# One decoder block on one core: products with norm factors, splits of the gates' fourth sums and the groups of weight sums placed at other points of the program

## The chip, the cores and the metric

The kernel runs on one core of one Trainium2 chip. The metric is the device time of one execution in microseconds. Its work lies on TensorE (PE: matmuls; PEld: loads of stationary weights), VectorE (DVE), ScalarE (ACT), GpSimd (POOL, which here fills buffers and issues software DMAs) and SyncE (SP, which issues the loads and the small stores in the order of its queue).

## The reference

One layer of a decoder on 512 tokens and 16 learned meta tokens in front of them, width 1024, float32:

```
u   = rmsnorm(x) @ w_in          # one projection for both mixers
o   = hgrn2(q, f, i) of 8 heads  # S_t = diag(f_t) S_(t-1) + (1 - f_t) i_t^T,  o_t = S_t^T q_t
o   = o * rsqrt(mean(o*o, of the head) + EPS) * norm_w * silu(g)
y   = mamba2(z, x, B, C, dt)     # 16 heads, 2 groups, gated norm
x   = x + concat(o, y) @ w_out
a,b = split(causal_conv3(rmsnorm(x) @ w_up))      # 2 x 2816
out = rmsnorm(x + (silu(a) * b) @ w_down), without the meta tokens
```

The change touches how o is normed and gated, how the weights of g and of w_up are prepared, and where their parts stand in the program.

## The kernel before, in words

Everything is kept with features on the 128 partitions and tokens along the row. Each float32 operand of a product is split into hi and lo parts, and a product is three matmuls into one accumulator: hi x hi, hi x lo, lo x hi (`product`, L327 to L341, and `mul`, L958 to L965). A weight block of 128 x 1024 takes this way: SyncE loads it into one of three `raw` buffers (L266 to L275 and L294), ScalarE copies it, rounded, into `whi` (L212), VectorE subtracts that from `raw` into `wlo` (L213), TensorE reads both. `ahead` keeps the stream two blocks ahead of its use, in the order of the list `chunks`.

The stages are: projection and Mamba mixer (to about 205 us), HGRN heads 0 to 7 (to about 412), the gates g0 to g3 (to about 487), the output rows (to about 530), the up products (to about 755), the down products. The output rows' first halves (`add_row`) are computed among the HGRN heads, behind heads 1 and 2 (`ROWS`).

*Sums of weights and of tokens.* Gates and most up pairs use a scheme of seven products instead of eight half-size products (L980 to L1021 for a gate, `scheme` for a pair, called W). It needs sums of weight halves and sums of token halves. The weights' sums are made in DRAM by accumulating software DMAs of GpSimd (`weight_sums`, L232 to L258): for each pair, copies, two rounds of adds and a last one. The pairs are worked off in GROUPS, and each group starts on a *tick*: VectorE copies one element of a named tile, GpSimd waits for it. The three 256-wide column blocks of a scheme's weights come through `raw` (w0, w2, w1); the fourth sum, 512 wide, has a tile of its own, s4, loaded on SyncE (L273) and split by `split_half` into s4h on ScalarE and s4l on VectorE (L221, L222). The tokens' sums (`normed_sums` with `token_sums`: `un`, `t_u`, t0, t1) are four sets, k = 0 to 3, and are made behind the HGRN heads that USUMS names.

*An HGRN head* (`hgrn_head`) takes three projections (f, q, v), makes decays and the decayed copies of q and k on VectorE (the last of them is kC, L816), and then small products: v and k transposed into pv, pk, pm and copied out by ScalarE (vt L830, mt L829, kt L831, mt's masked part by VectorE, L854), state updates (S), and o. mt is read by TensorE at L835 and L867.

*The norm of o.* Behind heads 3 and 7, `hgrn_norm` squares four heads' o, sums over features on TensorE, takes logarithm and exponential on ScalarE (with table loads), writes the factors of each head to DRAM (rs_d, L891) and reads them back over all partitions (rb, L893), both on SyncE. `hgrn_scale` multiplies o by the factor and the norm's weight, four instructions on VectorE (L898): for heads 0 to 3 behind head 4, for heads 4 to 7 behind gate 0.

*A gate* g_i serves heads 2i and 2i+1: banks x and z (pgt), y and v (pyvg for gate 0, pyg and pvg later). x takes w0's first half; y is seeded from x (L970, ScalarE); x goes on with w0's second half; y takes w2's first half; z is seeded from y (L970); v, z and y take the other halves; VectorE adds (sgv, L1016 and L1017), ScalarE takes silu (L1018); z takes s4 (h4, l4); silu of x and z (L1021); o is multiplied by both and split (oa_hi, oa_lo).

*What sets the order.* Each engine has its own queue and runs it in order. The order is found by a list scheduler with a model of durations. What is written under `first()` has priority; `tc.issue_after(x)` keeps instructions from being placed ahead of x; otherwise the place in the program decides among what is ready. Buffers with a tag are handed out in rings: a tile's first writer waits until the last reader of the tile that held the buffer is done.

Of the kernel before, what the change touches and what calls it, by code (L numbers as in the profile page):

```python
# [19 lines left out]
T0 = META - 2  # L20
# [36 lines left out]
NG = NH // 2  # L57
GROUPS = [("g", i) for i in range(NG)], WS[0:5], WS[5:10], WS[10:13], WS[13:], [("dn", 1)], [("dn", 2)], [("dn", 3)]
HT = 258
USUMS = {4: (0,), 5: (1, 2), 6: (3,)}  # L60
ROWS = {1: range(0, 4), 2: range(4, 8)}
# [6 lines left out]
def tile_block(ctx: ExitStack, tc: tile.TileContext, xT, w_in, w_dt, w_out, w_up, w_down,  # L68
# [148 lines left out]

    last_s4 = []

# [40 lines left out]
    def scheme_weights(key):  # L260

        kind, j = key
        raw = raw_tile(key)
        hi, lo = split_tiles(key)
        if kind == "w0":
            nc.sync.dma_start(raw[:], pair_of(j)[0])  # L266
        elif kind == "w2":
            nc.sync.dma_start(raw[:], sumd[j][:, 0:2 * HK])
        else:
            n = "_".join(map(str, j)) if isinstance(j, tuple) else j  # L270
            tag = "m" if isinstance(j, tuple) else "ab"
            s4 = slot(f"s4_{n}", 512, tag=tag)
            nc.sync.dma_start(s4[:], sumd[j][:, 3 * HK:])  # L273
            nc.sync.dma_start(raw[:, 0:HK], sumd[j][:, 2 * HK:3 * HK])
            nc.sync.dma_start(raw[:, HK:], pair_of(j)[1][:, HK:])  # L275
        split_weights(raw, hi, lo, slice(0, 2 * HK), V)
        if kind != "w1":
            return hi, lo
        h4, l4 = slot(f"s4h_{n}", 512, F32R, tag=tag), slot(f"s4l_{n}", 512, F32R, tag=tag)
        last_s4[:] = [split_half(s4[:], h4[:], l4[:])]  # L280
        return hi, lo, h4, l4

    def ahead(n):
        while wnext[0] < min(n, len(chunks)):
            key, src, kc = chunks[wnext[0]]
            if key[0] in ("w0", "w1", "w2"):
                with first():
                    wdone[key] = scheme_weights(key)
                wnext[0] += 1
                continue  # L290
            with first(), ExitStack() as st:
                raw, hi, lo = raw_tiles(key)
                d = slice(0, kc * P)
                nc.sync.dma_start(raw[:, d], src() if callable(src) else src)  # L294
                if key[0] == "dn" and key[1] < 2 and not key[2]:
                    st.enter_context(tc.issue_after(last_s4[0].ins))
                split_weights(raw, hi, lo, d, V)
            wdone[key] = (hi, lo)
            wnext[0] += 1
# [314 lines left out]
    def mamba_heads(g):  # L614
# [4 lines left out]
        def decays(h):  # L619
# [11 lines left out]
            if h == 1:  # L631
                weight_sums(GROUPS[6], L)

# [73 lines left out]
    mamba_states(0)  # L707
    weight_sums(GROUPS[5], rstd1)
    next_phase(LOGS)
# [44 lines left out]
    os_ = []  # L754
    weight_sums(GROUPS[1], ys[7])

    def hgrn_head(h):
# [52 lines left out]
        def packed(t, c):  # L810
            return t.rearrange("p (a c t) -> p a c t", c=c, t=16)
# [3 lines left out]
        V.tensor_tensor(packed(qC, 4), vw(q_, 128, 64), part(1, 8, 4), ALU.mult)  # L815
        V.tensor_tensor(packed(kC, 4), vw(k_, 128, 0), part(4, 8, 0), ALU.mult)  # L816

# [76 lines left out]

    def hgrn_scale(h0):
        for h in range(h0, h0 + 4):
            o, rb = os_[h], rbs[h]
            V.scalar_tensor_tensor(o[:, T0:], o[:, T0:], col(C_HN + h), rb[:, T0:], ALU.mult, ALU.mult)  # L898

# [34 lines left out]
    def normed_sums(k):  # L934

        fs = []
        for kk in (k, k + KD // 2):
            t = slot(f"un{kk}", tag="L")
            V.tensor_tensor(t[:, T0:], uh[kk][:, T0:].bitcast(F32), ul[kk][:, T0:].bitcast(F32), ALU.add)
            fs += [t[:, c] for c in tails]  # L940
        uts.append(token_sums(f"u{k}", fs, "L", lambda: next(uplaces)))

    for h in range(NH):
        hgrn_head(h)
        for j in ROWS.get(h, ()):
            add_row(j, 1, obh, obl)
            if j == 3:
                weight_sums(GROUPS[2], hs[j])
        if h == 4:
            hgrn_scale(0)  # L950
        if h % 4 == 3:
            hgrn_norm(h - 3)
        for k in USUMS.get(h, ()):
            normed_sums(k)
        if h == 4:
            weight_sums(GROUPS[3], os_[h])

# [9 lines left out]
    def seed(ps, of):  # L967

        with evac():
            A.activation(ps, of, AF.Copy)  # L970

# [11 lines left out]
    for i in range(NG):  # L983
# [23 lines left out]
        mul(y, w2h[:, 0:HK], w2l[:, 0:HK], t2)  # L1007
        seed(z, y)
        w1h, w1l, h4, l4 = weights("w1", key)
        mul(v, w1h[:, 0:HK], w1l[:, 0:HK], t3, True)  # L1010
# [4 lines left out]
        with evac():  # L1015
            V.tensor_tensor(sv[:, B_], s7[:], z, ALU.add)  # L1016
            V.tensor_tensor(sv[:, A_], s7[:], y, ALU.add)  # L1017
            A.activation(sv[:], sv[:], AF.Silu, scale=-1.0)  # L1018
# [3 lines left out]
        for h, g in ((2 * i, sg), (2 * i + 1, sv)):  # L1022
# [8 lines left out]
            oal.append(lo)  # L1031
        if i == 0:
            hgrn_scale(4)
    weight_sums(GROUPS[4], os_[6])

# [159 lines left out]
    for j in range(KF):  # L1195
# [10 lines left out]
        if j == 20:  # L1206
            weight_sums(GROUPS[7], ac)
        for i in STEPS.get(j, ()):
# [212 lines left out]
```

## Time and profile before

| what | us |
|---|---|
| median of three runs (lowest, highest) | 886.75 (883.96, 887.15) |
| profiled execution | 888.65 |
| its span, first to last instruction | 886.9 |
| TensorE busy | 849.8 |
| VectorE, ScalarE busy | 643.0, 500.6 |
| POOL busy | 138.6 |
| mean granted clock of TensorE | 0.981 of full |

The span ends 1.75 us short of the profiled execution's time. A row of a timeline gives the start in us, the length in us, engine, line, operation, output <- inputs, partitions x elements, and in brackets the idle time of the engine ahead of it with what ended it. A wait is put down to the operation that ended it. A row of a table of stretches gives the stretch, its length, busy us and instruction counts of PE, PEld, DVE, ACT and POOL, then the granted clock (1.00 is full), the DMA engines' mean busy share and GB/s.

### The profile page before, as it was taken

To read this page: it belongs to the slowest core of one execution; us is meant where nothing else is said; L and a number is where in the kernel's file an instruction comes from. 1 tells how busy PE (TensorE), PEld (TensorE's weight loads), DVE (VectorE), ACT (ScalarE), POOL (GpSimd) and SP (SyncE) were. 2 spreads that over 40 slices of the span, in tenths; PEclk is the share of its full clock that TensorE was granted. 3 is DMA by queue.
4 is the path that set the end of the run, shared out by engine and by line. 5 is a ranking of instruction groups with operands and counts; after the bars stand their busy time and mean duration, and the time that the engine had idled before them with its cause. 6 is when DMAs were issued, how large, how long until landed. Compare 5 with 4: busy or idle time off the path is not lost. (4 is left out here: it accounts for less than half of the span.)

```text
span 886.9 us, 17039 instructions
## 1 busy us (share of the span) xinstructions
PE 849.8 (96%) x6864; PEld 817.4 (92%) x6864; DVE 643.0 (73%) x1106; ACT 500.6 (56%) x805; POOL 138.6 (16%) x182
## 2 busy tenths in 40 slices
PE   6999999999999997998979999999999999999996
PEld 6998898999999997997869999989999999889985
DVE  6985968788463666975456668987988888985535
ACT  8628875965242362553635545556767667764433
POOL 1310221223212322232200221300000000100000
PEclk9999999999999997998879999999999999999999
DMA  7484799896988988899874997965555555845543
GB/s 250 159 206 147 210 286 238 166 158 208 255 163 170 297 199 178 162 198 239 179 178 154 292 219 147 197 170 192 187 178 188 178 192 168 209 119 154 156 137 125
DMA packets 65839, 168.73 MB, mean 190 GB/s; under 512 B 6856, under 2 KB 11336, under 8 KB 65760
## 3 DMA queue, kind: packets, MB, share of 16 engines
q0 software_dynamic: 24800, 62.53, 35.7%
q1 hardware_dynamic: 38432, 101.52, 35.6%
q10 hardware_dynamic: 2528, 3.60, 1.2%
q8 instruction: 54, 0.88, 0.4%
q14 instruction: 25, 0.20, 0.1%
HBM read 165.47 MB, written 64.67 MB: 259 GB/s over the span
## 5 line engine op out<-in xcount | busy, mean ns | idle before, releaser
L340 PE MATMUL pj<-u_hi,whi_in 128*128 128x272 f32 (+1 forms) x624 | 132.9, 292 | 0.1
L340 PE MATMUL pj<-u_lo,whi_in 128*128 128x272 f32 (+1 forms) x624 | 131.4, 290 | 0.0
L340 PE MATMUL pj<-u_hi,wlo_in 128*128 128x272 f32 (+1 forms) x624 | 129.5, 287 | 0.0
L340 PEld LDWEIGHTS pj<-u_hi,whi_in 128*128 128x128 f32 x624 | 97.6, 190 | 3.2 <-issue 2.7
L340 PEld LDWEIGHTS pj<-u_lo,whi_in 128*128 128x128 f32 x624 | 97.6, 190 | 2.1 <-issue 1.8
L340 PEld LDWEIGHTS pj<-u_hi,wlo_in 128*128 128x128 f32 x624 | 97.5, 191 | 1.4 <-issue 1.3
L212 ACT ACTIVATE whi_in<-raw_in 128x1024 fp32r<-128x1024 f32 (+1 forms) x50 | 47.6, 952 | 74.2 <-PE pj L340 47.0
L213 DVE TENSOR_TENSOR wlo_in<-raw_in,whi_in 128x1024 fp32r<-128x1024 f32 (+1 forms) x50 | 54.6, 1092 | 26.0 <-ACT whi_in L212 21.7
L212 ACT ACTIVATE whi_w<-raw_w 128x1024 fp32r<-128x1024 f32 x54 | 57.1, 1057 | 28.2 <-PE pup L964 13.5
L213 DVE TENSOR_TENSOR wlo_w<-raw_w,whi_w 128x1024 fp32r<-128x1024 f32 x54 | 65.9, 1221 | 6.7 <-ACT whi_w L212 6.3
L237 POOL COPY tick<-ticks 128x1 f32<-128x1 f32 x8 | 10.8, 1346 | 293.3 <-DVE ticks L236 293.3
L213 DVE TENSOR_TENSOR wlo_d<-raw_d,whi_d 128x768 fp32r<-128x768 f32 x21 | 20.1, 958 | 29.8 <-ACT whi_d L212 29.8
L965 PE MATMUL pup<-n_hi,wlo_w 128*128 128x258 f32 x144 | 40.7, 283 | 0.5 <-DVE wlo_w L213 0.5
L963 PE MATMUL psn<-t1h,whi_w 128*128 128x258 f32 x144 | 40.9, 284 | 0.0
L963 PE MATMUL pup<-n_hi,whi_w 128*128 128x258 f32 x144 | 40.8, 283 | 0.0
L964 PE MATMUL psn<-t1l,whi_w 128*128 128x258 f32 x144 | 40.8, 283 | 0.0
L965 PE MATMUL psn<-t1h,wlo_w 128*128 128x258 f32 x144 | 40.6, 282 | 0.0
L964 PE MATMUL pup<-n_lo,whi_w 128*128 128x258 f32 x144 | 40.5, 281 | 0.0
L253 POOL DMA_DIRECT2D sums<-in_w_up_dram x18 | 21.2, 1178 | 113.8 <-issue 113.8
L212 ACT ACTIVATE whi_d<-raw_d 128x768 fp32r<-128x768 f32 x21 | 17.8, 846 | 32.1 <-PE pup L1248 14.3
L911 DVE TENSOR_TENSOR xr<-xr,pout 128x514 f32<-128x514 f32 x16 | 11.0, 689 | 32.7 <-PE pout L340 32.7
L212 ACT ACTIVATE whi_out<-raw_out 128x1024 fp32r<-128x1024 f32 x16 | 16.9, 1058 | 25.4 <-PE pj L340 14.4
(578 smaller groups left out, 2844.4 us busy)
## 6 DMA issues: line engine op xcount, KB each, us to landing
sums<-in_w_up_dram POOLq DMA_DIRECT2D x54, 512.0 KB, 8.4
raw_in<-in_w_in_dram SPq DMA_DIRECT2D x42, 512.0 KB, 5.1
sums<-in_w_up_dram POOLq DMA_DIRECT2D x36, 256.0 KB, 8.3
raw_w<-in_w_up_dram SPq DMA_DIRECT2D x18, 512.0 KB, 3.6
raw_w<-sums SPq DMA_DIRECT2D x18, 512.0 KB, 3.7
raw_out<-in_w_out_dram SPq DMA_DIRECT2D x16, 512.0 KB, 6.9
sumsdn<-in_w_down_dram POOLq DMA_DIRECT2D x9, 768.0 KB, 7.8
sumsg<-in_w_in_dram POOLq DMA_DIRECT2D x12, 512.0 KB, 9.2
```

The lines of the kernel that those rows point to most:

```text
L212: A.activation(hi[:, d], raw[:, d], AF.Copy)
L213: eng.tensor_tensor(lo[:, d], raw[:, d], hi[:, d].bitcast(F32), ALU.subtract)
L237: gate = G.tensor_copy(tick[:], ticks[:, n:n + 1])
L253: G.dma_start(ds[j][:, 0:2], of[j][3], accum_op=ALU.add)
L340: PE.matmul(ps[:, O + a0:O + a1], w, x[:, a0:a1], start=s, stop=e)
L911: V.tensor_tensor(hs[j][:, T0:], hs[j][:, T0:], ps[:, O + T0:O + NT], ALU.add)
L963: PE.matmul(ps, wh, xh, start=first, stop=False, skip_group_check=True)
L964: PE.matmul(ps, wh, xl, start=False, stop=False, skip_group_check=True)
L965: last_product[:] = [PE.matmul(ps, wl, xh, start=False, stop=k == KD // 2 - 1, skip_group_check=True)]
```

## The change

It has five parts. The up pairs' groups become 5, 7 and 6 pairs where they were 5, 5, 3 and 5; the group that started behind head 4 is gone. The token sums come behind heads 2 and 3, two sets each, and their temporaries take the tag "y" instead of "L". The products with norm factors of heads 0 to 3 are kept behind head 4's last kC product; those of heads 4 to 7 stand behind gate 1, after the addition of its A half. The split of a gate's fourth sum moves from the load to behind z's seed, with h4 and l4 in the tag "ab". And the loads of the up pairs' fourth sums are kept behind the load of an output row's weights, ("out", 1, 0).

```diff
-GROUPS = [("g", i) for i in range(NG)], WS[0:5], WS[5:10], WS[10:13], WS[13:], [("dn", 1)], [("dn", 2)], [("dn", 3)]
+GROUPS = [("g", i) for i in range(NG)], WS[0:5], WS[5:12], WS[12:], [("dn", 1)], [("dn", 2)], [("dn", 3)]
-USUMS = {4: (0,), 5: (1, 2), 6: (3,)}
+USUMS = {2: (0, 1), 3: (2, 3)}
...
-            tag = "m" if isinstance(j, tuple) else "ab"
-            s4 = slot(f"s4_{n}", 512, tag=tag)
-            nc.sync.dma_start(s4[:], sumd[j][:, 3 * HK:])
+            s4 = slot(f"s4_{n}", 512, tag="m" if isinstance(j, tuple) else "ab")
+            with ExitStack() as st:
+                for i in hold:
+                    st.enter_context(tc.issue_after(i.ins))
+                nc.sync.dma_start(s4[:], sumd[j][:, 3 * HK:])
...
-        h4, l4 = slot(f"s4h_{n}", 512, F32R, tag=tag), slot(f"s4l_{n}", 512, F32R, tag=tag)
+        if isinstance(j, tuple):
+            return hi, lo, s4
+        h4, l4 = slot(f"s4h_{n}", 512, F32R, tag="ab"), slot(f"s4l_{n}", 512, F32R, tag="ab")
...
+                if key == ("out", 1, 0):
+                    hold[:] = [load]
...
-        V.tensor_tensor(packed(kC, 4), vw(k_, 128, 0), part(4, 8, 0), ALU.mult)
+        keys[h] = V.tensor_tensor(packed(kC, 4), vw(k_, 128, 0), part(4, 8, 0), ALU.mult)
...
-    def hgrn_scale(h0):
-        for h in range(h0, h0 + 4):
-            o, rb = os_[h], rbs[h]
-            V.scalar_tensor_tensor(o[:, T0:], o[:, T0:], col(C_HN + h), rb[:, T0:], ALU.mult, ALU.mult)
+    def hgrn_scale(h0, behind):
+        with tc.issue_after(behind.ins):
+            for h in range(h0, h0 + 4):
+                o, rb = os_[h], rbs[h]
+                V.scalar_tensor_tensor(o[:, T0:], o[:, T0:], col(C_HN + h), rb[:, T0:], ALU.mult, ALU.mult)
...
-            t = slot(f"un{kk}", tag="L")
+            t = slot(f"un{kk}", tag="y")
...
         if h == 4:
-            hgrn_scale(0)
+            hgrn_scale(0, keys[4])
...
-        if h == 4:
-            weight_sums(GROUPS[3], os_[h])
...
-        seed(z, y)
-        w1h, w1l, h4, l4 = weights("w1", key)
+        seeded = seed(z, y)
+        w1h, w1l, s4 = weights("w1", key)
+        h4, l4 = slot(f"s4h_g{i}", 512, F32R, tag="ab"), slot(f"s4l_g{i}", 512, F32R, tag="ab")
+        with first(), tc.issue_after(seeded.ins):
+            split_half(s4[:], h4[:], l4[:])
...
-            V.tensor_tensor(sv[:, A_], s7[:], y, ALU.add)
+            added = V.tensor_tensor(sv[:, A_], s7[:], y, ALU.add)
...
-        if i == 0:
-            hgrn_scale(4)
-    weight_sums(GROUPS[4], os_[6])
+        if i == 1:
+            hgrn_scale(4, added)
+    weight_sums(GROUPS[3], os_[6])
```

The other lines of the diff renumber the down pairs' groups. What it moves is shown at three places.

ScalarE at the end of head 7, before: the split of gate 0's fourth sum (s4h_g from s_g) directly behind the last head's v.

```order
L212 ACTIVATE whi_w_(g_5108<-raw_w_(g0)_5107 128x1024
L771 ACTIVATE v_4972<-pj_4923 128x528
L221 ACTIVATE s4h_g_5116<-s_g_5110 128x512
L830 ACTIVATE vt_5020<-pv_5008 128x512
L829 ACTIVATE mt_2245<-pm_5010 16x256
L831 ACTIVATE kt_5021<-pk_5009 128x384
L970 ACTIVATE pyvg_5103<-pgt_5102 128x258
L839 ACTIVATE S_5026<-pS_5025 128x128
```

The same place of the changed kernel:

```order
L212 ACTIVATE whi_w_(g_5099<-raw_w_(g0)_5098 128x1024
L779 ACTIVATE v_4963<-pj_4914 128x528
L838 ACTIVATE vt_5011<-pv_4999 128x512
L837 ACTIVATE mt_2245<-pm_5001 16x256
L839 ACTIVATE kt_5012<-pk_5000 128x384
L977 ACTIVATE pyvg_5094<-pgt_5093 128x258
L847 ACTIVATE S_5017<-pS_5016 128x128
L877 ACTIVATE o_5056<-pm_5001 128x2
L212 ACTIVATE whi_w_(g_5135<-raw_w_(g1)_5134 128x1024
L977 ACTIVATE pgt_5093<-pyvg_5094 128x258
L221 ACTIVATE s4h_g_5159<-s_g_5101 128x512
L878 ACTIVATE o_5056<-po_5046 128x512
```

The split has moved from ahead of vt, mt and kt to behind both seeds of gate 0 (pyvg from pgt, pgt from pyvg) and behind the first weights of gate 1.

VectorE between gates 0 and 1, before (o from o, pt and rb is the product with a norm factor; wlo_w of g2 are gate 2's weights):

```order
L222 TENSOR_TENSOR oa_lo<-o_2569,oa_hi 128x514
L222 TENSOR_TENSOR oa_lo<-o_2835,oa_hi 128x514
L898 SCALAR_TENSOR_TENSOR o_4168<-o_4168,pt,rb_5091 128x514
L213 TENSOR_TENSOR wlo_w_(g_5289<-raw_w_(g2)_5287,whi_w_(g_5288 128x1024
L898 SCALAR_TENSOR_TENSOR o_4479<-o_4479,pt,rb_5094 128x514
L222 TENSOR_TENSOR s4l_g_5257<-s_g_5250,s4h_g_5256 128x512
L1016 TENSOR_TENSOR sgv_5245<-sg_5246,pgt_5241 128x258
L898 SCALAR_TENSOR_TENSOR o_4781<-o_4781,pt,rb_5097 128x514
L898 SCALAR_TENSOR_TENSOR o_5065<-o_5065,pt,rb_5100 128x514
L213 TENSOR_TENSOR wlo_w_(g_5308<-raw_w_(g2)_5306,whi_w_(g_5307 128x1024
```

The same place of the changed kernel:

```order
L222 TENSOR_TENSOR oa_lo<-o_2569,oa_hi 128x514
L222 TENSOR_TENSOR oa_lo<-o_2835,oa_hi 128x514
L213 TENSOR_TENSOR wlo_w_(g_5272<-raw_w_(g2)_5270,whi_w_(g_5271 128x1024
L222 TENSOR_TENSOR s4l_g_5296<-s_g_5237,s4h_g_5295 128x512
L1026 TENSOR_TENSOR sgv_5232<-sg_5233,pgt_5228 128x258
L213 TENSOR_TENSOR wlo_w_(g_5291<-raw_w_(g2)_5289,whi_w_(g_5290 128x1024
L1027 TENSOR_TENSOR sgv_5232<-sg_5233,pyg 128x258
L907 SCALAR_TENSOR_TENSOR o_4254<-o_4254,pt,rb_5082 128x514
L907 SCALAR_TENSOR_TENSOR o_4524<-o_4524,pt,rb_5085 128x514
L907 SCALAR_TENSOR_TENSOR o_4790<-o_4790,pt,rb_5088 128x514
L907 SCALAR_TENSOR_TENSOR o_5056<-o_5056,pt,rb_5091 128x514
L213 TENSOR_TENSOR wlo_w_(g_5375<-raw_w_(g2)_5373,whi_w_(g_5374 128x1024
```

The four products now stand together behind gate 1's two additions (sgv), and two of gate 2's three splits ahead of them, the third behind.

VectorE in head 4, before (mt from maskA and pm is the masked part of the transpose that TensorE reads):

```order
L898 SCALAR_TENSOR_TENSOR o_3370<-o_3370,pt,rb_3900 128x514
L939 TENSOR_TENSOR un_4175<-u_hi,u_lo 128x514
L939 TENSOR_TENSOR un_4177<-u_hi,u_lo 128x514
L918 TENSOR_TENSOR t_u_4179<-un_4175 128x258
L920 TENSOR_TENSOR t_u_4179<-un_4177,un_4175 128x258
L898 SCALAR_TENSOR_TENSOR o_3868<-o_3868,pt,rb_3903 128x514
L919 SCALAR_TENSOR_TENSOR t_u_4180<-un_4177,t_u_4179 128x258
L939 TENSOR_TENSOR un_4482<-u_hi,u_lo 128x514
L222 TENSOR_TENSOR t0l_u_4186<-t_u_4179,t0h_u_4185 128x516
L921 SCALAR_TENSOR_TENSOR t_u_4180<-t_u_4180,un_4177 128x258
L854 COPY_PREDICATED mt_2244<-maskA,pm_4113 16x2
L213 TENSOR_TENSOR wlo_in_4276<-raw_in_4274,whi_in_4275 128x1024
```

The same place of the changed kernel:

```order
L213 TENSOR_TENSOR wlo_in_4263<-raw_in_4261,whi_in_4262 128x1024
L928 SCALAR_TENSOR_TENSOR t_u_3978<-un_3975,t_u_3977 128x258
L222 TENSOR_TENSOR t0l_u_3984<-t_u_3977,t0h_u_3983 128x516
L907 SCALAR_TENSOR_TENSOR o_2569<-o_2569,pt,rb_3944 128x514
L930 SCALAR_TENSOR_TENSOR t_u_3978<-t_u_3978,un_3975 128x258
L907 SCALAR_TENSOR_TENSOR o_2835<-o_2835,pt,rb_3947 128x514
L907 SCALAR_TENSOR_TENSOR o_3384<-o_3384,pt,rb_3950 128x514
L222 TENSOR_TENSOR t1l_u_3988<-t_u_3978,t1h_u_3987 128x516
L907 SCALAR_TENSOR_TENSOR o_3918<-o_3918,pt,rb_3953 128x514
L213 TENSOR_TENSOR wlo_in_4321<-raw_in_4319,whi_in_4320 128x1024
L862 COPY_PREDICATED mt_2244<-maskA,pm_4199 16x2
L862 COPY_PREDICATED mt_2244<-maskA,pm_4199 16x2
```

The four products stand at the same place of the head; between the last of them and mt there were four pieces of the token sums (t_u, un, t0l_u), and there is now one weight split.

More of the change, by code (lines that the diff above doesn't have):

```diff
@@ L216, in tile_block @@
     sumd = {}
-    last_s4 = []
+    last_s4, hold = [], []
     def split_half(x, hi, lo):
@@ L293, in ahead @@
                 d = slice(0, kc * P)
-                nc.sync.dma_start(raw[:, d], src() if callable(src) else src)
+                load = nc.sync.dma_start(raw[:, d], src() if callable(src) else src)
+                if key == ("out", 1, 0):
+                    hold[:] = [load]
                 if key[0] == "dn" and key[1] < 2 and not key[2]:
@@ L631, in decays @@
             if h == 1:
-                weight_sums(GROUPS[6], L)
+                weight_sums(GROUPS[5], L)
         def outputs(t):
@@ L707, in tile_block @@
     mamba_states(0)
-    weight_sums(GROUPS[5], rstd1)
+    weight_sums(GROUPS[4], rstd1)
     next_phase(LOGS)
@@ L755, in tile_block @@
     weight_sums(GROUPS[1], ys[7])
+    keys = {}
     def hgrn_head(h):
@@ L937, in normed_sums @@
         for kk in (k, k + KD // 2):
-            t = slot(f"un{kk}", tag="L")
+            t = slot(f"un{kk}", tag="y")
             V.tensor_tensor(t[:, T0:], uh[kk][:, T0:].bitcast(F32), ul[kk][:, T0:].bitcast(F32), ALU.add)
             fs += [t[:, c] for c in tails]
-        uts.append(token_sums(f"u{k}", fs, "L", lambda: next(uplaces)))
+        uts.append(token_sums(f"u{k}", fs, "y", lambda: next(uplaces)))
     for h in range(NH):
@@ L969, in seed @@
         with evac():
-            A.activation(ps, of, AF.Copy)
+            return A.activation(ps, of, AF.Copy)
     def mark(ps, w, x):
@@ L1206, in tile_block @@
         if j == 20:
-            weight_sums(GROUPS[7], ac)
+            weight_sums(GROUPS[6], ac)
         for i in STEPS.get(j, ()):
```

## The prediction

> **What bounds the kernel now.** I read the page's busy shares and slices first, then TensorE's waits, then tables of stretches around the longest waits, and at last the timelines of the engines that TensorE waited for. Busy shares and the granted clock by slice:
>
> ```profile
> span 886.9 us, 17039 instructions
> PE 849.8 (96%) x6864; PEld 817.4 (92%) x6864; DVE 643.0 (73%) x1106; ACT 500.6 (56%) x805; POOL 138.6 (16%) x182
> PEclk9999999999999997998879999999999999999999
> ```
>
> TensorE is busy for 96%, so a change that takes no matmul away can win only what lies in its idle time and in the slices where the clock falls below 9: slices 16 to 21 of 40, that is about 340 to 490 us. The longest waits of TensorE (total, count, longest, us):
>
> ```profile
> PE pm L867 <- DVE mt L854: 5.6, 1, 5.6
> PE pS L835 <- ACT mt L829: 4.2, 1, 4.2
> PE pgt L965 <- DVE wlo_w_(g L213: 3.4, 1, 3.4
> PE pgt L963 <- DVE sgv L1016: 1.7, 1, 1.7
> PE pgt L963 <- ACT pyg L970: 1.6, 1, 1.6
> PE pvg L965 <- DVE wlo_w_(g L213: 1.4, 1, 1.4
> PE pout L340 <- ACT sg L1021: 0.7, 1, 0.7
> ```
>
> These lie where the change moves work: the first (I call it A) in head 4, the second (B) between head 7 and gate 0, the other four up to the 1.4 (C) in gates 1 and 2: 1.6 + 3.4 + 1.7 + 1.4 = 8.1 us; the 0.7 comes at the first output row. Behind A, B and C the clock is at one half (stretch; length; PE busy, instructions; the last three columns are clock, DMA share, GB/s):
>
> ```profile
> 347.70:354.40 6.70, 6.64 (x31) 6.64 (x32) 6.64 (x18) 1.42 (x3) 2.05 (x2) 0.50 0.83 163
> 416.60:425.90 9.30, 9.27 (x53) 8.69 (x54) 3.52 (x9) 2.44 (x6) 2.53 (x3) 0.50 0.72 110
> 455.10:463.60 8.50, 7.00 (x31) 6.74 (x32) 6.64 (x11) 3.91 (x7) 0.00 (x0) 0.50 0.56 191
> ```
>
> What that costs is seen on one kind of matmul, in pairs of which one starts after the other, behind A and after the clock is back:
>
> ```profile
> 349.21 0.63 PE L340 MATMUL pj<-u_hi,wlo_in 128*128 128x258 f32 x2
> 349.64 0.63 PE L340 MATMUL pj<-u_hi,whi_in 128*128 128x258 f32 x2
> 354.62 0.40 PE L340 MATMUL pj<-u_hi,whi_in 128*128 128x258 f32 x2
> 354.86 0.40 PE L340 MATMUL pj<-u_lo,whi_in 128*128 128x258 f32 x2
> ```
>
> A pair takes 0.43 us there and 0.24 us here, so a busy microsecond at half clock loses 1 - 0.24/0.43 = 0.44 us: 6.64 x 0.44 = 2.9 us behind A, 9.27 x 0.44 = 4.1 behind B, 7.00 x 0.44 = 3.1 behind C. All that can be won is then A 8.5, B 8.3 and C 11.2, together 28 us.
>
> **The change part by part.** *Split of gate 0's fourth sum (B).* ScalarE's timeline at the end of head 7, and TensorE's first matmul behind it:
>
> ```profile
> 410.51 0.59 ACT L771 ACTIVATE v<-pj 128x528 f32<-128x528 f32 x1
> 415.21 0.63 ACT L221 ACTIVATE s4h_g<-s_g 128x512 fp32r<-128x512 f32 x1 [4.11 <-DMA s_g<-sumsg]
> 416.23 0.36 ACT L829 ACTIVATE mt<-pm 16x256 f32<-16x256 f32 x1
> 416.63 0.58 PE L835 MATMUL pS<-mt 128*128 128x128 f32 x1 [4.21 <-ACT mt L829]
> ```
>
> s4h_g waits 4.11 us for its load, and vt, mt and kt, which the last head needs, stand behind it in ScalarE's order. In the changed order s4h_g comes after seed z, behind vt, mt, kt and the first seeds. Then mt follows v by what TensorE needs for the transposes; I leave 0.7 us of idle time of the 4.21, and with so short a gap no half clock: -3.5 - 4.1 = -7.6. Its load lands where it did; its first reader, the product into z, stands several products later, which is its cover. Were the cover gone, it would cost what is left of those 4.11 us. Bounds: -4.2 (the idle part goes, some other gap of the seeds keeps the clock down) to -8.3.
>
> *Products with norm factors in gates (C).* VectorE's and ScalarE's rows, and SyncE's loads that they wait for:
>
> ```profile
> 450.04 0.75 DVE L898 SCALAR_TENSOR_TENSOR o<-o,pt,rb 128x514 f32<-128x514 f32 x1 [5.41 <-DMA rb<-rs_d]
> 450.71 1.22 DVE L213 TENSOR_TENSOR wlo_w_(g<-raw_w_(g2)_5287,whi_w_(g 128x1024 fp32r<-128x1024 f32 x1
> 453.32 0.63 ACT L221 ACTIVATE s4h_g<-s_g 128x512 fp32r<-128x512 f32 x1 [7.98 <-DMA s_g<-sumsg]
> 413.04 11.66 SPq L273 DMA_DIRECT2D s<-sums  x2
> 443.14 0.32 SPq L273 DMA_DIRECT2D s_g<-sumsg  x1
> rb<-rs_d SPq DMA_DIRECT2D x8, 257.0 KB, 6.6
> ```
>
> The first weights of gate 2 wait on VectorE behind a product that waits 5.41 us for its broadcast factor; after the change all four products stand behind the addition of gate 1's A half, so that these weights, both halves of gate 1's fourth sum and the sgv additions go ahead of them. The price moves: gate 2's third split (wlo of w1) now stands behind the four products, 4 x 0.75 = 3.0 us of VectorE, and waits for the last factor. Its reader comes after two products of gate 2, so I count 1.3 us there. Gate 1's fourth sum: its load left at 443.14 and its split ran at 453.32, 10.2 us later, beside four broadcasts and three loads of up sums, two of which held SyncE for 11.66 us. Those three loads now stand behind the output rows' weights and the software DMA has nothing left to do here, so I expect it some 5 us sooner, which is 0 to 1.5 us late for TensorE once 3.4 us of waiting ahead of it are gone: 0.8. With some 0.8 for the table loads' gap (1.6 before) and 1.6 for two small ones (each 0.4 to 1.4 before), 4.5 us of C's 11.2 remain, if the clock stays up; I take -7. Bounds: 0 (the waits only move) and -9.
>
> *Products with norm factors in head 4 (A).* The two last of them and what stands behind, VectorE, and TensorE's wait:
>
> ```profile
> 341.01 0.75 DVE L898 SCALAR_TENSOR_TENSOR o<-o,pt,rb 128x514 f32<-128x514 f32 x1 [2.46 <-DMA rb<-rs_d]
> 345.01 0.75 DVE L898 SCALAR_TENSOR_TENSOR o<-o,pt,rb 128x514 f32<-128x514 f32 x1 [1.35 <-DMA rb<-rs_d]
> 347.56 0.14 DVE L854 COPY_PREDICATED mt<-maskA,pm 16x2 f32<-16x2 int32 x1
> 347.63 1.21 DVE L213 TENSOR_TENSOR wlo_in<-raw_in,whi_in 128x1024 fp32r<-128x1024 f32 x1
> 347.76 0.37 PE L867 MATMUL pm<-mt 128*128 128x2 f32 x1 [5.59 <-DVE mt L854]
> ```
>
> Here the edit does less than its words: the bound is head 4's last kC product, and the order places the four products at nearly the same place as before, still ahead of mt. The wait for rb, which ends with the fourth, is untouched; between it and mt four pieces of the sums' work (345.76 to 347.56, 1.8 us) are replaced by one weight split of 1.21. On ScalarE one more small activation of the sums comes ahead of the norm's logarithm: factors about 0.5 us later, an estimate by one such activation. So mt stays near 347.5. On TensorE 14 matmuls that stood behind its first reader now stand ahead of it: 14 x 0.12 = 1.7 us of the wait are filled. I take -2.0 and keep the half clock, for 3.6 us would remain and 3.44 us (with 1.72 after it) was followed by half clock at C. Bounds: 0 (factors later by 1.7) to -8.5 (they land in time).
> [...]
>
> *Token sums sooner and their tag.* The same instructions, now in heads 2 to 4 and ahead of the gates by more; VectorE has room there (73%). Nothing; against 1 us if they push a head's own work.
>
> *Groups 5, 7, 6.* Software DMA is long ahead of need in the heads. The last group has six pairs in place of five and begins after the gates as before. Its price is seen where the last one drains:
>
> ```profile
> sums<-in_w_up_dram POOLq DMA_DIRECT2D x54, 512.0 KB, 8.4
> 565.00:600.00 35.00, 33.19 (x270) 32.34 (x269) 28.08 (x44) 19.51 (x30) 4.35 (x6) 1.00 0.76 181
> ```
>
> 1.81 us of idle in 35; another pair lasts about two such adds, 17 us, so 0 to 0.9 more, and its own readers come far later: 0.
>
> *Held loads of the up pairs' fourth sums.* Gate 3's end and what stands around the held load:
>
> ```profile
> 485.53 0.60 ACT L1021 ACTIVATE sg<-pgt 128x516 f32<-128x516 f32 x1 [3.18 <-PE pgt L965]
> 481.15 1.79 SPq L294 DMA_DIRECT2D raw_out<-in_w_out_dram  x2
> 494.38 0.33 SPq L306 DMA_DIRECT2D raw_up<-in_w_up_dram  x1
> s<-sums SPq DMA_DIRECT2D x18, 256.0 KB, 4.0
> raw_out<-in_w_out_dram SPq DMA_DIRECT2D x16, 512.0 KB, 6.9
> ```
>
> Two of these splits now stand on ScalarE just ahead of the last gate's sg and of its second oa_hi. The load leaves behind the first of the two raw_out at 481.15, about 481.5, and lands at 485.5 by its own median of 4.0 or at 488.4 by its neighbours' 6.9: sg, at 485.53 before, is 0.6 to 3.5 us late. I take +1.5, nearer to the own row; from 3.4 us of idle on, half clock would add up to 4.
>
> **Sum.** -7.6 - 7 - 2.0 + 1.5 = -15.1. The profiled execution took 888.65 us, 1.75 around its span; the median of the three runs is 886.75 (883.96 to 887.15). So 873.5 for an execution like the profiled one, 871.6 for the median. I predict 871.6.
>
> **Rivals.**
> 1. *The gates' waits only move.* The late broadcast stops the third split in place of the first, and gate 1's fourth sum is split ahead of gate 2's weights: C gains nothing. For it: each factor lands 6.6 us after issue whatever stands behind it, and SyncE waits in order. Against: the readers of what is now late come later. -7.6 - 2.0 + 1.5 = -8.1: 878.6.
> 2. *A goes wholly.* With the norm's loads earlier by some 2.5 us, or the half clock missed: -8.5 in place of -2.0: -21.6, 865.1. For it: three of four products land before 342. Against: nothing in the order brings the fourth factor forward.
> 3. *Slower: SyncE stops at the sixth pair's held load.* In the new order the load of the third up pair's fourth sum (s_6) waits for a free buffer on SyncE, with raw_up and the last two raw_out behind it. Before, raw_up left at 494.38. If s_6 leaves d us later than that, the stream of three weight buffers starves TensorE by d and the clock drops: d + 4.1 - 15.1, over no change from d = 11 and slower by 0.5% from d = 15.4. A buffer that comes free only with the first up product, about 25 us later, gives +14: 901. Against it: SyncE's wait there is for VectorE and for loads, not for TensorE, so the buffer's last reader is a split.
> 4. *All of it at once small*: A nothing, B only idle (-4.2), C nothing, +1.5: -2.7, 884.
>
> **How the numbers follow.** Forecast 0.52, rival 1 0.23, rival 2 0.14, rival 3 0.04, rival 4 0.07. A difference under 0.5% (4.4 us) can't be told from none. Faster by more: forecast, rivals 1 and 2 = 0.89; same: rival 4 = 0.07; slower 0.04. The forecast's own range is 867 to 876: down by 4.3, half of the 6.5 and 2 that A and C could still give, up by 4.5, the held loads' 2.0 and A's and C's remainders at 2.5 more; rival 1 with its spread goes to 881, and of rival 2 the lower half lies below 863. The range 863 to 881 leaves out rivals 3 and 4 and half of rival 2: 0.18.
>
> **What would show it.** In the waits after: pS behind mt under 1 us and no slice at half clock behind 416; pgt behind wlo_w_(g gone, a new wait for pvg or for s4h_g of under 2; pm behind mt still near 3.6, with half clock behind. A wait over 3 us of pout or oa_hi's readers at the output rows would make me wrong upward; a missing wait A downward. Half clock anywhere between 415 and 480 says that C's remainder is larger than I put it.

## The result, and the profile after

The changed kernel took 874.18 us (median of four runs, 872.70 to 874.94), the kernel before 886.95 (median of four, 883.96 to 889.86): ratio 0.985, 95% interval 0.982 to 0.989. That is 12.8 us, where 15.1 had been forecast; the profiled executions, 888.65 and 873.74, differ by 14.9. The page of the changed kernel:

```profile
span 872.0 us, 17031 instructions
PE 844.8 (97%) x6864; PEld 811.9 (93%) x6864; DVE 642.8 (74%) x1105; ACT 500.9 (57%) x805; POOL 138.8 (16%) x181
PEclk9999999999999999899999999999999999999999
```

The engines do the same work. TensorE is 5.0 us less busy for the same 6864 matmuls, which goes with the clock: four slices below 9 before, one now. Its waits in and around the heads and gates:

```profile
PE pm L875 <- DVE mt L862: 6.7, 1, 6.7
PE pS L843 <- ACT mt L837: 0.4, 1, 0.4
PE pvg L972 <- DVE wlo_w_(g L213: 0.8, 1, 0.8
PE pgt L970 <- ACT pyg L977: 0.6, 1, 0.6
PE pout L346 <- ACT sg L1031: 0.8, 1, 0.8
PE p L970 <- ACT whi_w L212: 1.4, 1, 1.4
```

B (pS behind mt) is gone from 4.2 to 0.4, and C from four waits of 8.1 us to two of 1.4. A (pm behind mt) is still there and has grown from 5.6 to 6.7. The output row's wait is as it was, and in the up stage stands a new wait of 1.4 for a weight copy. Stretches of the changed kernel (columns as before: length, busy of PE, PEld, DVE, ACT, POOL, then clock, DMA share, GB/s):

```profile
350.80:356.00 5.20, 5.17 (x24) 5.17 (x25) 5.14 (x12) 0.22 (x2) 1.17 (x2) 0.50 0.83 173
413.60:426.00 12.40, 12.37 (x112) 10.86 (x113) 4.80 (x10) 5.83 (x11) 3.88 (x5) 1.00 0.97 195
426.00:440.00 14.00, 13.24 (x102) 12.15 (x101) 7.68 (x12) 11.27 (x18) 0.00 (x0) 1.00 0.61 172
440.00:464.00 24.00, 23.41 (x194) 23.13 (x193) 19.60 (x32) 16.30 (x25) 0.00 (x0) 1.00 0.61 195
```

In these stages half clock is left behind A alone; from 413 to 464 the clock is 1.00 throughout.

Wait A shows how a factor comes. ScalarE, SyncE, VectorE and TensorE of the changed kernel in head 4:

```profile
329.24 0.69 ACT L145 ACTIVATE rh<-ph,eps 128x512 f32<-128x512 f32 x1 [1.46 <-PE phm L894]
332.05 0.87 SPq L899 DMA_DIRECT2D rs_d<-rh  x3
335.89 1.30 SPq L901 DMA_DIRECT2D rb<-rs_d  x3
337.24 0.28 SPq L899 DMA_DIRECT2D rs_d<-rh  x1
341.55 0.32 SPq L901 DMA_DIRECT2D rb<-rs_d  x1
348.83 0.75 DVE L907 SCALAR_TENSOR_TENSOR o<-o,pt,rb 128x514 f32<-128x514 f32 x1 [3.60 <-DMA rb<-rs_d]
349.50 1.22 DVE L213 TENSOR_TENSOR wlo_in<-raw_in,whi_in 128x1024 fp32r<-128x1024 f32 x1
350.64 0.14 DVE L862 COPY_PREDICATED mt<-maskA,pm 16x2 f32<-16x2 int32 x1
350.83 0.59 PE L875 MATMUL pm<-mt 128*128 128x2 f32 x2 [6.74 <-DVE mt L862]
```

ScalarE's logarithm for the norm (rh) waits 1.46 us for TensorE's sums of the squares and starts 1.2 us later than before (329.24 for 328.02). The first three read-backs (rb) leave 3.8 us after their stores (rs_d), where before it was 1.2 (330.84 to 332.05), and the last store stands behind them on SyncE. So the last factor is stored at 337.24, read back from 341.55 and there at 348.83, 3.8 us later than before (345.01). mt starts 1.8 us after that product does, where it was 2.6 with the token sums between. TensorE reaches its place at 344.10, 1.9 us later than before, and waits longer all the same.

In gate 1 it went the other way. Gate 1's fourth sum:

```profile
434.48 0.34 SPq L275 DMA_DIRECT2D s_g<-sumsg  x1
438.91 0.63 ACT L221 ACTIVATE s4h_g<-s_g 128x512 fp32r<-128x512 f32 x1 [1.35 <-DMA s_g<-sumsg]
```

4.4 us from issue to split, 10.2 before. The changed kernel's software DMA issued its last add at 422.78, and the trace has its last packet at 428.42, so that nothing of it ran beside this load.

### The profile page after: what moved, and what is told of

Its sections match the earlier page's. It is cut to its first block, busy times and chain, and to the rows that moved or that the text cites. A ratio compares the mean times of both kernels' runs of the same rounds, so it can differ in the third digit from the quotient of the medians.

```text
span 872.0 us, 17031 instructions
## 1 busy us (share of the span) xinstructions
PE 844.8 (97%) x6864; PEld 811.9 (93%) x6864; DVE 642.8 (74%) x1105; ACT 500.9 (57%) x805; POOL 138.8 (16%) x181
## 4 chain that ended last, share of the span: by engine, by line
PE 91%; DMA 4%; DVE 2%; ACT 1%; issue 1%; SPq 0%; DVEq 0%; ACTq 0%
PE pj L346 28%; PE pout L346 10%; PE pup L346 5%; PE pup L970 4%; PE pup L972 4%; PE pup L971 4%; PE psn L971 2%; PE psn L972 2%; PE psn L970 2%; PE pup L1257 2%; PE pup L1258 2%; PE pup L1259 2%; PE pdn L1274 1%; PE pdn L1275 1%; PE pdn L1276 1%; DMA raw_w<-in_w_up_dram 1%
## 5 line engine op out<-in xcount | busy, mean ns | idle before, releaser
L346 PE MATMUL pj<-u_hi,whi_in 128*128 128x272 f32 (+1 forms) x624 | 131.1, 290 | 0.0
L237 POOL COPY tick<-ticks 128x1 f32<-128x1 f32 x7 | 10.5, 1500 | 283.8 <-DVE ticks L236 283.8
```

What stands on the lines that cost most here:

```text
L237: gate = G.tensor_copy(tick[:], ticks[:, n:n + 1])
L346: PE.matmul(ps[:, O + a0:O + a1], w, x[:, a0:a1], start=s, stop=e)
```

## The experiments

Twelve more kernels ran, each with the kernel before on the same chip; the ratio is to that kernel. A trace shows one execution, a ratio the median of several. Two theories were put against each other. *Order*: each wait belongs to what stands in one engine's queue behind an instruction that waits for a load; putting it elsewhere removes the wait. *Loads*: the waits go because SyncE and the DMA engines have less to do in the gates, and so loads land sooner.

| kernel | median, us | before there | ratio (95%) |
|---|---|---|---|
| changed kernel | 874.18 | 886.95 | 0.985 (0.982 to 0.989) |
| p_split: split alone | 883.75 | 886.92 | 0.997 (0.994 to 0.999) |
| p_scale4: products of heads 4 to 7 alone | 883.67 | 886.92 | 0.996 (0.994 to 0.999) |
| u_hold: changed, no hold | 874.36 | 886.92 | 0.985 (0.979 to 0.992) |
| u_split: changed, split at load | 881.77 | 888.37 | 0.993 (0.991 to 0.996) |
| u_scale4: changed, products behind gate 0 | 880.02 | 888.37 | 0.992 (0.989 to 0.995) |
| u_groups: changed, groups 5, 5, 3, 5 | 880.86 | 888.37 | 0.992 (0.990 to 0.994) |
| u_sums: changed, token sums late | 877.62 | 888.37 | 0.990 (0.987 to 0.992) |
| s_head5: changed, products of heads 0 to 3 behind head 5 | 871.73 | 886.92 | 0.983 (0.976 to 0.989) |
| u_groups_early: u_groups, gate 1's fourth sum loaded early | 876.53 | 888.04 | 0.988 (0.985 to 0.991) |
| s_early: s_head5, the same early load | 870.94 | 888.04 | 0.980 (0.976 to 0.984) |
| s_head5_567: s_head5, groups 5, 6, 7 | 864.69 | 888.04 | 0.974 (0.971 to 0.976) |
| s_early_567: both | 865.23 | 888.04 | 0.975 (0.972 to 0.978) |

### One part alone: p_split and p_scale4

The kernel before with the split behind z's seed (the other lines hand the seed and s4 on):

```diff
-        seed(z, y)
-        w1h, w1l, h4, l4 = weights("w1", key)
+        seeded = seed(z, y)
+        w1h, w1l, s4 = weights("w1", key)
+        ...
+        with first(), tc.issue_after(seeded.ins):
+            split_half(s4[:], h4[:], l4[:])
```

> The kernel before with one part of the change: a gate's fourth sum is split behind z's seed. Theory 1 (order: each wait belongs to what stands in one engine's queue behind a late load): the wait of pS for mt falls from 4.2 to under 1 us and the half clock behind it goes, 7.5 us in all: 879.3 us for 886.8; A (5.6 us at pm) and C (8.1 us in gates 1 and 2) stay. Theory 2 (loads: the waits go because SyncE and the DMA engines have less to do there): s_g lands as late as before and holds up the next reader instead: the gain is under 4 us, 883 or more.

TensorE's long waits in p_split:

```profile
348.66 0.59 PE L869 MATMUL pm<-mt 128*128 128x2 f32 x2 [6.99 <-DVE mt L856]
445.99 0.55 PE L965 MATMUL pgt<-u_hi,s4h_g 128*128 128x258 f32 x1 [5.08 <-DVE sgv L1021]
453.73 0.58 PE L967 MATMUL pvg<-t0h_u,wlo_w_(g 128*128 128x258 f32 x1 [4.39 <-DVE wlo_w_(g L213]
```

Wait B is gone (0.4 us are left), as *order* said, yet the ratio gives 3.1 us and not 7.5: gate 1's fourth sum and gate 2's weights now cost 5.1 and 4.4 us. TensorE comes to that fourth sum 12.5 us sooner (440.91 for 453.43), and the sum is split only 9.2 us sooner (444.15 for 453.32). So the order removes its wait, but part of the gain is waited for again at the next load. The time lies where *loads* had put it (883 or more), though not for its reason: gate 0's fourth sum holds up nothing more. A is 1.4 us longer as well, but the order of every engine up to the end of A is that of the kernel before, so the edit's order can't be the cause. The run has a side effect too: its three loads of up sums leave from 475.44 on, behind the gates' loads, although the hold is not in this kernel.

The kernel before with the products behind gate 1:

```diff
-            V.tensor_tensor(sv[:, A_], s7[:], y, ALU.add)
+            added = V.tensor_tensor(sv[:, A_], s7[:], y, ALU.add)
...
-        if i == 0:
-            hgrn_scale(4)
+        if i == 1:
+            with tc.issue_after(added.ins):
+                hgrn_scale(4)
```

> The kernel before with one part of the change: the products with norm factors of heads 4 to 7 stand behind gate 1's additions. Theory 1 (order): the 3.4 us for wlo of gate 2 go, with part of the half clock; 5 to 7 us of C's 11.2: about 881. Theory 2 (loads): gate 1's fourth sum still lands at about 453, behind three loads of up sums on SyncE, so that TensorE waits for s4h_g instead: 0 to 2 us, 885 or more. B (4.2 us at pS) stays by both.

```profile
350.72 0.59 PE L867 MATMUL pm<-mt 128*128 128x2 f32 x2 [7.61 <-DVE mt L854]
416.00 0.49 PE L835 MATMUL pS<-mt 128*128 128x128 f32 x2 [1.87 <-ACT mt L829]
431.83 0.62 PE L885 MATMUL ph<-osq,cf 128*32 128x512 f32 x1 [3.54 <-ACT osq L884]
450.61 0.36 PE L963 MATMUL pgt<-u_hi,s4h_g 128*128 128x258 f32 x1 [1.44 <-DVE sgv L1016]
```

The 3.4 us for gate 2's weights are gone; but a wait of 3.5 has come at the norm's squares, and A is 2.0 longer, again with the order of the kernel before up to there (but for one pair on VectorE far ahead). B shrank to 1.9, though its edit isn't in this kernel: these waits also hang on when TensorE and the load arrive. By the ratio 3.5 us came of it, a time between the two expectations (the profiled execution took 880.31 us, the median is 883.67). The two parts alone give 6.6 us, the whole change, with its other three parts, 12.8.

### One part undone: u_split, u_scale4, u_groups, u_sums, u_hold

> The changed kernel with the gates' fourth sums split at their load again, as before. Theory 1 (order): wait B comes back, 4.2 us at pS with 4.1 of half clock, less the 0.4 left there now: 882 for 874.2, if gate 0's fourth sum lands where it did. Theory 2 (loads): with SyncE and the software DMA freed the load lands in time: 874 to 877.

```profile
351.90 0.59 PE L873 MATMUL pm<-mt 128*128 128x2 f32 x2 [7.66 <-DVE mt L860]
419.06 0.49 PE L841 MATMUL pS<-mt 128*128 128x128 f32 x2 [4.27 <-ACT mt L835]
```

B is back at 4.27: gate 0's fourth sum takes 8.4 us from issue to split (409.27 to 417.64), as before (8.3), and only the order keeps that from mattering. By the ratios the split is worth 7.0 us ((0.9933 - 0.9854) x 888); *order* stands here. What a freed DMA would do for this load is not tested: the second group's adds are issued until 426.98, so they still run beside it.

The products go behind gate 0 again, with no addition to wait for (`if i == 0: hgrn_scale(4, keys[7])`).

> The changed kernel with the products with norm factors of heads 4 to 7 behind gate 0 again. Theory 1 (order): gate 2's first split waits for a factor on VectorE again, 2 to 3.4 us with half clock: 878 to 880. Theory 2 (loads): the factors now land so much sooner that nothing waits: 874 to 875.

```profile
447.86 0.39 PE L972 MATMUL pvg<-t0h_u,wlo_w_(g 128*128 128x258 f32 x1 [2.31 <-DVE wlo_w_(g L213]
588.83 0.39 PE L970 MATMUL p<-t0h,whi_w 128*128 128x258 f32 x1 [2.32 <-ACT whi_w L212]
```

A weight split waits in gate 2, 2.3 us, and the clock stays at 1.00 behind it; by the ratios 5.8 us are lost, but the gates show only part of it: A is 7.4 us here, and there is a wait of 2.3 in the up stage. Both of these also differ between kernels whose order is the same there (u_hold, below), so where the rest of the 5.8 lies stays open.

```diff
-GROUPS = [...], WS[0:5], WS[5:12], WS[12:], ...
+GROUPS = [...], WS[0:5], WS[5:10], WS[10:13], WS[13:], ...
...
+        if h == 4:
+            weight_sums(GROUPS[3], os_[h])
```

The other lines renumber the groups behind.

> The changed kernel with the up pairs' sums in groups of 5, 5, 3, 5 again, the third started in head 4. Theory 1 (order): no change, 873 to 875.5. Theory 2 (loads): the software DMA of the third group lies beside gates 0 and 1 again, factors and fourth sums land some 2 us later, and 2 to 6 us come back: 876 to 880.

SyncE, ScalarE, TensorE and a stretch of u_groups:

```profile
436.03 0.34 SPq L275 DMA_DIRECT2D s_g<-sumsg  x1
450.70 0.63 ACT L221 ACTIVATE s4h_g<-s_g 128x512 fp32r<-128x512 f32 x1 [12.27 <-DMA s_g<-sumsg]
452.54 0.55 PE L972 MATMUL pgt<-u_hi,s4h_g 128*128 128x258 f32 x1 [9.68 <-DVE sgv L1028]
452.50:458.00 5.50, 5.46 (x26) 5.49 (x27) 5.50 (x8) 2.24 (x4) 0.00 (x0) 0.52 0.34 106
```

Nothing of VectorE's or ScalarE's order in the gates has changed, and TensorE waits 9.7 us for a load that takes 14.7 us instead of 4.4, with the third group's adds issued until 445.38. By the ratios 6.0 us are lost. *Loads* stands here: the groups, which the forecast held for worth nothing, carry the end of C. The waits of this trace are longer than the loss, for two reasons: it is of an execution of 885.08 us, where the median is 880.86, and A is 9.4 us in it (in heads 3 and 4 the order does differ).

> The changed kernel with the token sums behind heads 4, 5 and 6 and in the tag L again. Theory 1 (order): no part of the gain rests on them but wait A, 6.7 us now and 5.6 before: a split less stands ahead of the norm's table loads, so A is 1 us shorter: 873. Theory 2 (loads) says nothing of them. Their rival: sums in heads 5 and 6 hold up a head's VectorE: 875 to 878.

```profile
353.21 0.59 PE L875 MATMUL pm<-mt 128*128 128x2 f32 x2 [10.77 <-DVE mt L862]
```

With the token sums late A is 10.8 us, 4.0 more. By the ratios 3.6 us are lost, but the intervals overlap (0.987 to 0.992, 0.982 to 0.989), so the loss is not clear of noise. The first expectation was wrong in sign. The time is the rival's (875 to 878), but its reason is not seen: the longer wait is in head 4.

> The changed kernel without the hold on the loads of the up pairs' fourth sums. Theory 1 (order): C stays gone, since VectorE's and ScalarE's order in the gates is what removed it: 874 to 876 for 874.2. Theory 2 (loads): three loads of up sums stand among the gates' loads again, SyncE is blocked on their sums, and C's waits come back: 879 to 882.

```profile
462.57 0.38 SPq L275 DMA_DIRECT2D s<-sums  x1
```

The ratio is that of the changed kernel, 0.985, and so is the order: on every engine the two traces have the same instructions in the same order from the first to the last. The first held load leaves at 462.57, in the changed kernel at 462.98. So the hold does nothing; the scheduler puts these loads behind the output rows' weights without it, and in p_split they stand behind the gates' loads too. The condition of *loads* did not come about, and this run does not test it. It is a repetition, and as such it tells something else: with nothing changed A is 6.3 us for 6.7, and the wait in the up stage 3.1 for 1.4.

### Wait A: s_head5

```diff
-        if h == 4:
-            hgrn_scale(0, keys[4])
+        if h == 5:
+            hgrn_scale(0, keys[5])
```

> The changed kernel with the products with norm factors of heads 0 to 3 placed one head later, behind head 5's last kC product. By theory 1 (order) wait A goes whole, 6.7 us of idle time and the half clock behind it, 2.9: 864.6 us for 874.2, with pm behind mt under 0.5 in all heads. Its rival: the wait moves to head 5 or the factors' buffers, held longer, hold up another tile: 0 to 3 us, 871 or more.

Its first long wait behind 300 us, with SyncE's and ScalarE's rows of that load and the stretch behind it:

```profile
439.50 0.55 PE L970 MATMUL pgt<-u_hi,s4h_g 128*128 128x258 f32 x1 [5.98 <-DVE sgv L1026]
429.00 0.34 SPq L275 DMA_DIRECT2D s_g<-sumsg  x1
437.67 0.63 ACT L221 ACTIVATE s4h_g<-s_g 128x512 fp32r<-128x512 f32 x1 [8.55 <-DMA s_g<-sumsg]
439.50:444.50 5.00, 5.00 (x23) 5.00 (x24) 5.00 (x7) 2.20 (x4) 0.00 (x0) 0.51 0.43 145
```

Wait A is gone and does not come back in head 5, and TensorE reaches gate 1's fourth sum 8.3 us sooner (433.52 for 441.81). But the group of seven pairs is not done sooner: its last add is issued at 426.62 (422.78 in the changed kernel), 2.4 us ahead of the fourth sum's load at 429.00, which takes 8.7 us; by the 5.2 to 11.0 us that an add took to land in s_early, it still ran beside this load. The time is the rival's (871 or more), the place of the new wait is not. The wait of 6.0 and its half clock take most of A's gain; the interval is too wide (0.976 to 0.989) to tell what is left of it.

### What the late load hangs on: u_groups_early, s_early, s_head5_567, s_early_567

Two ways to spare gate 1's fourth sum: its load ahead of the norm's stores, right behind gate 0's (`early`), or a shorter second group, so that the software DMA is done sooner (`567`). The lines left out make gate 1 take the tile that is loaded already.

```diff
...
+            if j == ("g", 0):
+                e4 = early[("g", 1)] = slot("s4_g_1", 512)
+                nc.sync.dma_start(e4[:], sumd[("g", 1)][:, 3 * HK:])
...
-WS[0:5], WS[5:12], WS[12:]
+WS[0:5], WS[5:11], WS[11:]
```

> The changed kernel with groups of 5, 5, 3, 5 again, and the load of gate 1's fourth sum issued ahead of the norm's stores, right behind gate 0's. If the groups' worth is only that this load lands late beside the software DMA (9.7 us of waiting, half clock behind it), the wait goes and the time is that of the changed kernel with some wait A more: 874 to 877. If the software DMA also holds up factors and weights there, less than half of it comes back: 879 or more.

```profile
449.82 0.58 PE L978 MATMUL pgt<-u_hi,whi_w_(g 128*128 128x258 f32 x1 [2.84 <-ACT whi_w_(g L212]
```

The wait of 9.7 is gone, one of 2.8 for gate 3's first weights is new; 3.7 us of the groups' 6.0 by the ratios are back, within the expected 874 to 877. That most of the groups' worth was this one load fits, but is not proven: A is 5.8 us in this trace and 9.4 in that of u_groups, with the same order up to there.

> The changed kernel with the products of heads 0 to 3 behind head 5, and gate 1's fourth sum loaded early. The 6.0 us that TensorE waited in gate 1 with the first of these edits alone, and some 3 us of half clock behind them, go: 863 to 865. Rival: another load that shares the stretch with the software DMA, the factors or gate 2's weights, takes the wait over: 868 or more.

```profile
433.96 0.82 SPq L907 DMA_DIRECT2D rb<-rs_d  x2
442.23 1.06 ACT L212 ACTIVATE whi_w_(g<-raw_w_(g3)_5407 128x1024 fp32r<-128x1024 f32 x1 [6.68 <-DMA raw_w_(g3)_5407<-in_w_in_dram]
443.34 0.58 PE L976 MATMUL pgt<-u_hi,whi_w_(g 128*128 128x258 f32 x1 [5.13 <-ACT whi_w_(g L212]
```

The fourth sum is no longer waited for, and gate 3's weights are, 5.1 us: their load stands on SyncE behind the last two factors, which left only at 433.96. The rival was right in that another load takes the wait over, and in the time, but this load does not share its stretch with the software DMA: the last add in this trace is issued at 422.55, the load at 434.87, 12.3 us later, and an add takes at most 11.0 us to land. Sparing one load passes the wait to the next in SyncE's queue.

> The changed kernel with the products of heads 0 to 3 behind head 5, and groups of 5, 6, 7. The second group's software DMA ends some 18 us sooner, ahead of gate 1, so the fourth sum lands in about 4 us as in the changed kernel: the wait of 6.0 us and the half clock go, 863 to 865. Rival: the seventh pair at the end costs the up products what it gains here: 868 or more.

SyncE and ScalarE of that load, and the summary of the core:

```profile
424.68 0.34 SPq L275 DMA_DIRECT2D s_g<-sumsg  x1
430.16 0.63 ACT L221 ACTIVATE s4h_g<-s_g 128x512 fp32r<-128x512 f32 x1 [2.39 <-DMA s_g<-sumsg]
core 0: 863.8 us, clock 0.998
```

The last add of the group is issued at 408.48, the fourth sum takes 5.5 us, and no wait over 1.3 us is left between 300 and 600 us. 864.69 us, as forecast; against the changed kernel's own ratio the further gain is 1.2% of 888, 10.5 us. It is the fastest of all kernels run.

> Both edits beside the products behind head 5: groups of 5, 6, 7 and gate 1's fourth sum loaded early. If one of them is enough, as the theory has it, the second adds nothing: 863 to 865, within 1.5 us of either alone. If both carry a part, it is the fastest by 2 us or more.

The same time within the intervals (0.975 and 0.974): with the group short enough the early load adds nothing. The reverse, which the expectation had as well, does not hold: the early load alone is 870.94.

## Why the prediction was right, point by point

**B, forecast -7.6.** Right in mechanism and size: 4.2 us of idle time became 0.4 and half clock over 9.3 us became full, -7.9 by the two traces; undoing it alone costs 7.0 by the ratios.

**C, forecast -7 of 11.2.** The mechanism was right, and more of it went: of the four waits, 8.1 us, and the smaller one behind them, 1.4 us are left and no half clock, where 4.5 had been left standing. The third split of gate 2, behind four products now, had been put at 1.3 us and the fourth sum at 0.8; neither is waited for in the trace. The forecast also named the software DMA as the reason for the fourth sum's late load, which u_groups showed: 4.4 us with the group done, 14.7 beside it. It named the three loads of up sums too; they did leave gates 0 and 1, but no run keeps them there with the rest of the change, so their share stays open.

**A, forecast -2.0.** Here the step failed. It took the time at which the last factor lands as before with some 0.5 us added, and filled 1.7 us of the wait with 14 matmuls. TensorE did come 1.9 us later; the factor came 3.8 us later. The wait is 1.2 longer, and with the half clock behind it (5.2 us long instead of 6.7) A gave nothing. The forecast's own work between the product and mt did shrink (2.6 to 1.8 us). What it had no room for is how far the factor's way through store and read-back varies: A was 5.6 to 10.8 us in all kernels that kept the products in head 4. The order decides only part of that. Up to the end of A, p_split and p_scale4 have the order of the kernel before (but for that one pair on VectorE), with A at 5.6, 7.0 and 7.6 us; u_hold, u_scale4 and u_split have that of the changed kernel, with A at 6.7, 6.3, 7.4 and 7.7. So the growth by 1.2 us is within what one order gives, and what is shown is only that A did not shrink by 2.0. What sets the DMA's pace in each execution was not tested.

**Held loads, forecast +1.5.** The output row's wait went from 0.7 to 0.8. The load took 4.1 us to its split (462.98 to 467.11), as its own row had it. But TensorE's last product of the gate ended only at 467.43, so that sg, behind that split, was hardly held up (it starts at 467.65): the term was too large. Its 3.4 us from which half clock would follow were an estimate from gate 2's wait of 3.44 us; in s_early_567 half clock followed a wait of 1.86. And the loads' new place, which the forecast put down to the hold, does not come from it, as u_hold shows.

**Groups, forecast 0.** By its own part of the sum wrong: 6.0 us hang on them. But the gain lies in C, where the forecast had counted it; the accounts were set against the wrong edit.

**Token sums, forecast 0.** u_sums loses 3.6 us by the ratios, which is not clear of noise; its trace has A 4.0 us longer.

**The sum.** -7.9 for B, for C -8.8 of idle time with 1.4 left and -3.1 of half clock, -10.5, about +0.5 for A and +0.1 at the output row, +1.4 for a new wait in the up stage: -16.4, against -14.9 between the profiled executions. Followed by the same matmuls in both traces, the changed kernel is 0.9 us ahead before head 3, 0.8 behind at head 7's transposes, 17.5 ahead after 4194 of the 6864 matmuls (530.05 before, 512.56 after) and 14.9 at the end. So the gates give 18.3, as in this sum; heads 3 to 6 cost 1.7 where the sum has 0.5, and what follows costs 2.6 where it has 1.4. Between the medians it is -12.8. The forecast of 871.6 was 2.6 us too low: it gave A what A did not give, and C too little, and these nearly cancelled. That part of its closeness is luck. Two readings were off without touching the sum: slices 16 to 21 are 333 to 466 us, not 340 to 490, and the list of the longest waits leaves out the longest, 6.5 us at the program's start.

**The rivals.** That the gates' waits only move was not seen in the changed kernel, but it is what p_split, u_groups and s_head5 show: there they moved. That A goes wholly did not happen, and the stop of SyncE at the sixth pair's load neither.

## What to carry to other kernels

An instruction that waits for a load in an engine's ordered queue delays what stands behind it (4.11 us on ScalarE became 4.21 us on TensorE at B): place it behind the work that TensorE needs next, and look at the order that comes out, not at the words of the edit. But removing a wait makes TensorE arrive sooner at the next load, while the long run of background DMA was not done sooner (in s_head5 TensorE came to gate 1's fourth sum 8.3 us sooner, and the last add was issued 3.8 us later); such an edit can be worth less alone than inside the whole (3.1 and 3.5 us alone, 7.0 and 5.8 when undone, with intervals that overlap), and the background run has to be shortened with it, as s_head5 and s_head5_567 show (2.5 us beyond the changed kernel, not resolved, and 10.5). And a wait in one trace is one execution's: before a difference of 2 us is put down to an edit, look whether kernels with the same order show it too.

## What the runs showed of the hardware

A 256 KB load, gate 1's fourth sum, took 4.4 to 5.5 us from issue to its reader where no software DMA ran beside it (changed kernel, s_head5_567), and 8.7, 10.2 and 14.7 us where software DMAs of the weights' sums did (s_head5, kernel before, u_groups).

In these traces the half clock did not follow from the length of one wait alone. A wait of 1.86 us in the up stage of s_early_567 was followed by half clock, one of 2.32 us at the same instruction in u_scale4 (its row stands above) was not. The stretches around the two, cut in steps of 3.41 us, three for each:

```profile
585.82 0.38 PE L976 MATMUL p<-t0h,whi_w 128*128 128x258 f32 x1 [1.86 <-ACT whi_w L212]
583.32:586.73 3.41, 1.55 (x13) 1.34 (x12) 1.52 (x3) 2.02 (x4) 0.81 (x1) 1.00 1.00 206
586.73:590.14 3.41, 3.41 (x18) 3.41 (x18) 3.41 (x6) 2.29 (x3) 0.81 (x1) 0.50 1.05 291
590.14:593.55 3.41, 3.41 (x30) 3.41 (x30) 1.98 (x4) 1.46 (x4) 0.82 (x1) 1.00 1.04 242
583.89:587.30 3.41, 2.62 (x22) 2.41 (x21) 1.17 (x2) 0.00 (x0) 0.82 (x1) 1.00 1.03 277
587.30:590.71 3.41, 1.88 (x15) 1.89 (x16) 1.91 (x3) 2.93 (x5) 0.00 (x0) 1.00 0.84 197
590.71:594.12 3.41, 3.41 (x30) 3.41 (x29) 3.41 (x5) 2.73 (x5) 0.00 (x0) 1.00 0.80 195
```

The steps are those of the clock granted in these traces. Between 300 and 600 us the fourteen traces have 21 stretches at half clock (none in s_head5_567). Where a trace has more than one, they start whole numbers of 3.41 us apart (in the kernel before at 344.17, 415.85 and 453.40, which is 21 and 11 steps; in p_split at 345.87 and 444.86, which is 29), and each of the 21 lasts 3.41 us (s_early_567), 6.83 (changed kernel), 10.24 (kernel before) or 13.65 (p_split), waits included. In the steps at full clock right ahead of the 21, TensorE was idle for between 1.82 us (u_sums) and the whole 3.41 (changed kernel); among the steps there that another at full clock followed, the most idle had 1.87 us (p_scale4), 1.80 (u_scale4) and 1.66 (changed kernel). The wait of 1.86 us lay whole in one step, and that of 2.32 was shared by two (0.79 and 1.53 us idle). What sets the steps was not tested.
